# Decoder step on one core: operands of the gated feed-forward layers built from half pairs, squares added by VectorE, later norm products, adding transfers in the last head

## The chip, the cores and the metric

The kernel runs on one NeuronCore of a Trainium2 chip. The metric is the device time of one execution in microseconds, the median of three runs. Everything the kernel does happens on that core's engines: TensorE (PE; its weight loads are shown apart as PEld), VectorE (DVE), ScalarE (ACT), GpSimd (POOL), and SyncE (SP), which mostly starts transfers. Each engine works through its own list of instructions in order. A scheduler fixes that order when the kernel is built, and semaphores hold an instruction until what it needs has been written or released.

## The reference, cut to what matters

The model has two layers with d = 1024. It runs over 512 prompt tokens and 8 × 4 sample tokens with the same weights, so 544 token columns in all.

```python
for i in range(2):
    h = rmsnorm(x, norm_mix[i])
    x = x + (short_conv_mixer(h) if i == 0 else retention_mixer(h))   # x: 544 x 1024
    x = x + swiglu(rmsnorm(x, norm_ffn[i]), w_gate, w_up, w_down)      # 1024 -> 2816 -> 1024
y = rmsnorm(x, final_norm)

def rmsnorm(x, g): return x * rsqrt(mean(x * x, -1) + 1e-6) * g
def swiglu(x, wg, wu, wd): return (silu(x @ wg) * (x @ wu)) @ wd
```

`short_conv_mixer` is a projection to 3 × 1024, a gated convolution of width 3, and a projection back with `conv_w_out`. `retention_mixer` has four heads; each ends in a projection with its part of `ret_w_out`, which is added to x. All of it is float32.

## The kernel before, in words

**Layout.** x stands transposed in eight tiles `x[0]` to `x[7]` of 128 features by 544 tokens. A float32 product is made of three faster ones: each operand is split in a high and a low part (`split`: ScalarE copies to the high part, line 186, VectorE subtracts it to get the low part, line 187), and TensorE adds high·high, low·high and high·low.

**Order of a layer.** The mixer ends in a projection whose result is added to x tile by tile (`residual`, line 267). In layer 0 the order of the tiles is `PAIRED` = 0, 4, 1, 5, 2, 6, 3, 7. In layer 1 it comes from the last head's `out_project`, whose weight pieces 0, 2, 1, 3 carry two tiles each, so 0, 1, 4, 5, 2, 3, 6, 7. Then the feed-forward part `ffn` begins. Its norm's factor is not applied to x: the products are made from x times the gain alone, and the factor `R` is multiplied in later (lines 587 and 589).

**Seven products in place of eight.** A gate or up product of a pair of weight columns is a `Job`: one step of Strassen's scheme in Winograd's form. x is cut in features (tile k with tile k + 4) and in tokens (two halves of 272), and `operands` makes seven operands of 272 columns from each pair: four blocks and three sums or differences of blocks. The list `OPERAND` says which of the seven each product takes. There are four pairs, so a product is four times three matrix instructions of 128 × 272 (line 471). The first job is run as product 1 (`begin`), then 5, 6, 2, 7 (`middle`), product 1 of the next job, then 4 and 3 (`end`). Between products of one job ScalarE copies the running sum out of its bank ("u1", "u2", "u3": a snapshot, line 529) before the next product is added on top of it.

**Building the operands.** For each pair, ScalarE writes gain times x for both tiles into a buffer `f` (line 568), VectorE makes two differences in place (lines 404 and 405), a split of five blocks (1360 columns) follows, then two more differences (407 and 408) and a split of two blocks (544). The work on a pair starts when both its tiles are there. Two buffers `f` take turns.

**The norm.** `square_sum` adds up the squares: ScalarE squares a tile into `sqlast`, and GpSimd adds it to `sqacc` (line 216); the last tile's is added by VectorE (line 212). `rms_scale` is a generator: five small products with a column of `mean_w` (line 245), then a power on GpSimd (line 221), four empty steps, then six products that spread the factor over the partitions (line 225), then a copy to `R` (line 257). `Job.product` of the first job takes one step of it after each pair's three instructions.

**Weights of a job.** `weights7` loads two pieces, makes four differences on VectorE (lines 429 to 432), and splits. Half of each loaded piece gets its low part from an adding transfer: ScalarE writes minus the high part (line 416), and GpSimd's queue starts a transfer that adds the weight from memory to it (line 417). `load_piece(..., adding=True)` does the same for a whole piece of 128 × 1024 with `split_adding`, which the code before never asks for in `out_project`.

**Order by hand.** `tc.issue_after(ins)` makes the scheduler put what follows after a given instruction; other than that the order is the scheduler's.

## Time and profile before

| | |
|---|---|
| median of 3 runs | 1477.4 us (1476.63 to 1478.4) |
| profiled execution, own time | 1477.55 us |
| its span, first to last instruction | 1475.8 us |
| TensorE busy | 1453.5 us, 98% |
| VectorE / ScalarE / GpSimd busy | 963.4 / 627.8 / 150.5 us |
| mean granted TensorE clock | 0.992 |
| feed-forward of layer 0 begins (first line-471 instruction) | 201.63 us |
| feed-forward of layer 1 begins | 1084.47 us |

Times on the trace count from the span's start. A row of the timeline gives the start, the duration, the engine, the line, the operation, and output and input with their sizes. A row of the stretches gives the stretch, its length, the busy time of each engine with the number of instructions in parentheses, the granted clock of TensorE (1.00 is full), the share of the transfer engines and GB/s.

### The profile page before, as it was taken

Reading aid. Unit: us, or ns where it says so; the run is one execution under the profiler, and the core shown is the slowest. Engines: PE = TensorE matmul, PEld = TensorE weight load, DVE = VectorE, ACT = ScalarE, POOL = GpSimd, SP = SyncE. Lnnn points to the kernel's source line nnn. Section 1 sums busy time; section 2 is a strip of 40 time slices with the busy share of each in tenths; the row PEclk is TensorE's granted clock in tenths of the full one; section 3 lists DMA queues with packets and bytes.
Section 4 is the critical chain, followed back from the end, with each engine's and each line's share of the span. In section 5 each row is a group of like instructions: output and inputs, shape, how many; then the busy total and the mean of one; then the engine's idle time right before and its main releaser. Section 6 shows DMA issues by size and latency. Waiting matters only on the chain.

```text
span 1475.8 us, 26203 instructions
## 1 busy us (share of the span) xinstructions
PE 1453.5 (98%) x10920; PEld 1381.1 (94%) x10920; DVE 963.4 (65%) x1472; ACT 627.8 (43%) x914; POOL 150.5 (10%) x180
## 2 busy tenths in 40 slices
PE   9999999999999999999999999999989999999997
PEld 9999989999999999888988988987779999999997
DVE  6645678847749656648546835835788857848645
ACT  5222457626526435241141223224366725526434
POOL 0100131101101003000000000000041101101002
PEclk9999999999999999999999999999989999999999
DMA  6222235635536435237234523713426635536432
GB/s 225 82 91 86 89 100 132 147 115 131 143 106 144 119 81 192 100 115 246 84 126 161 201 86 114 250 51 118 170 77 150 144 115 133 145 102 141 125 80 83
DMA packets 80263, 188.05 MB, mean 127 GB/s; under 512 B 7680, under 2 KB 24960, under 8 KB 80144
## 3 DMA queue, kind: packets, MB, share of 16 engines
q1 hardware_dynamic: 66576, 162.01, 33.6%
q0 software_dynamic: 12704, 23.15, 9.5%
q8 instruction: 85, 1.39, 0.4%
q10 hardware_dynamic: 864, 1.22, 0.2%
q14 instruction: 34, 0.28, 0.1%
HBM read 165.18 MB, written 21.18 MB: 126 GB/s over the span
## 4 chain that ended last, share of the span: by engine, by line
PE 88%; DVE 6%; DMA 1%; ACT 1%; POOL 1%; issue 1%; SPq 0%; DVEq 0%; POOLq 0%; ACTq 0%
PE mm L173 35%; PE sm L471 31%; PE sm L173 8%; PE sm L883 2%; PE sm L884 2%; PE sm L885 2%; PE sm L161 1%; PE sm L163 1%; PE sm L162 1%; DVE S L1115 1%; PE sm L1094 1%; DVE wl L187 1%; DMA w<-in_ffgu_dram 1%; DVE ol L187 1%; DMA S<-in_rets_dram 1%
## 5 line engine op out<-in xcount | busy, mean ns | idle before, releaser
L186 ACT ACTIVATE wh<-w 128x1024 fp32r<-128x1024 f32 (+4 forms) x142 | 132.7, 939 | 369.4 <-PE mm L173 222.4
L471 PE MATMUL sm<-oh,wh 128*128 128x272 f32 x704 | 204.6, 291 | 4.1 <-ACT oh L186 2.5
L471 PE MATMUL sm<-ol,wh 128*128 128x272 f32 x704 | 203.7, 290 | 0.9 <-DVE ol L187 0.9
L471 PE MATMUL sm<-oh,wl 128*128 128x272 f32 x704 | 203.6, 289 | 0.0
L173 PE MATMUL mm<-xh,wh 128*128 128x272 f32 x932 | 195.0, 290 | 0.2 <-ACT wh L186 0.2
L173 PE MATMUL mm<-xh,wl 128*128 128x272 f32 x932 | 192.6, 289 | 0.0
L173 PE MATMUL mm<-xl,wh 128*128 128x272 f32 x932 | 192.0, 287 | 0.0
L187 DVE TENSOR_TENSOR wl<-w,wh 128x1024 fp32r<-128x1024 f32 (+4 forms) x142 | 153.9, 1088 | 28.5 <-ACT wh L186 26.3
L267 DVE TENSOR_TENSOR x<-x,mm 128x544 f32<-128x544 f32 x91 | 65.4, 719 | 139.2 <-PE mm L173 139.1
L471 PE MATMUL sm<-oh,h 128*128 128x272 f32 x528 | 152.5, 289 | 1.3 <-ACT h L186 0.9
L471 PE MATMUL sm<-ol,h 128*128 128x272 f32 x528 | 152.3, 289 | 0.0
L471 PE MATMUL sm<-oh,l 128*128 128x272 f32 x528 | 151.9, 288 | 0.0
L173 PEld LDWEIGHTS mm<-xh,wh 128*128 128x128 f32 x932 | 146.4, 189 | 5.4 <-DVE wl L187 3.4
L173 PEld LDWEIGHTS mm<-xl,wh 128*128 128x128 f32 x932 | 146.0, 188 | 0.1
L173 PEld LDWEIGHTS mm<-xh,wl 128*128 128x128 f32 x932 | 145.3, 188 | 0.3
L471 PEld LDWEIGHTS sm<-oh,wh 128*128 128x128 f32 x704 | 133.8, 190 | 5.9 <-ACT oh L186 2.7
L417 POOL DMA_DIRECT2D wl<-in_ffgu_dram x88 | 76.6, 871 | 595.9 <-ACT wl L416 359.4
L471 PEld LDWEIGHTS sm<-ol,wh 128*128 128x128 f32 x704 | 133.1, 189 | 1.1 <-DVE ol L187 1.1
L471 PEld LDWEIGHTS sm<-oh,wl 128*128 128x128 f32 x704 | 133.6, 190 | 0.0
L414 ACT ACTIVATE wh<-w 128x1024 fp32r<-128x1024 f32 x88 | 93.2, 1059 | 70.7 <-PE sm L471 47.0
L471 PEld LDWEIGHTS sm<-oh,h 128*128 128x128 f32 x528 | 100.1, 190 | 1.8 <-ACT h L186 1.7
L187 DVE TENSOR_TENSOR l<-w,h 128x1024 fp32r<-128x1024 f32 x88 | 83.8, 954 | 24.6 <-ACT h L186 24.3
(258 smaller groups left out, 3115.2 us busy)
## 6 DMA issues: line engine op xcount, KB each, us to landing
w<-in_ffgu_dram SPq DMA_DIRECT2D x88, 512.0 KB, 3.9
wl<-in_ffgu_dram POOLq DMA_DIRECT2D x88, 256.0 KB, 4.6
w<-in_ffdn_dram SPq DMA_DIRECT2D x96, 192.0 KB, 2.5
S<-in_rets_dram SPq DMA_DIRECT2D x16, 1024.0 KB, 7.5
out_rets_dram<-S SPq DMA_DIRECT2D x16, 1024.0 KB, 5.4
w<-in_cvin_dram SPq DMA_DIRECT2D x21, 512.0 KB, 3.3
w<-in_rtqk_dram SPq DMA_DIRECT2D x16, 512.0 KB, 3.6
w<-in_rtv_dram SPq DMA_DIRECT2D x16, 512.0 KB, 3.6
```

Source lines behind the costliest of these rows:

```text
L161: nc.tensor.matmul(out, lh, rh, start=start, stop=False, skip_group_check=True)
L162: nc.tensor.matmul(out, lh, rl, start=False, stop=False, skip_group_check=True)
L173: last_product[0] = nc.tensor.matmul(half(pt, hf)[:, :HT], w[:, c], act[k][:, hf * HT : (hf + 1) * HT], start=(first and k == ks[0] and i ...
L186: h = nc.scalar.activation(dh, src, AF.Copy)
L187: nc.vector.tensor_sub(dl, src, dh.bitcast(F32))
L267: last_residual[0] = nc.vector.tensor_add(xk, xk, p)
L414: nc.scalar.activation(wh, w, AF.Copy)
L417: nc.gpsimd.dma_start(wl[:, n:], src[:, n:], accum_op=ALU.add)
L471: nc.tensor.matmul(out, w[:, c], b[k][:, at, :], start=(first and k == 0 and i == 0), stop=(k == n - 1 and i == 2), skip_group_check=True,)
L883: nc.tensor.matmul(out, xh[kt][:, ts_], wh[:, cw], start=(kt == 0), stop=False)
L884: nc.tensor.matmul(out, xh[kt][:, ts_], wl[:, cw], start=False, stop=False)
L885: nc.tensor.matmul(out, xl[kt][:, ts_], wh[:, cw], start=False, stop=(kt == KT - 1))
```

## The change

Six edits belong together.

1. `operands` is cut in two. `operands_left` works on the first tile of a pair alone: one difference, and a split of operands 0 and 1, which products 1 and 5 take. `operands_rest` works when the second tile is there: two differences and a split of three operands, then one difference and a split of two. `OPERAND` is renumbered to suit. A pair has the same number of columns to split, in three pieces (544, 816, 544) instead of two (1360, 544).
2. The order of tiles in layer 0 becomes 0, 4, 1, 5, 2, 3, 6, 7, so tile 3, the first of the last pair, comes before tiles 6 and 7.
3. All squares are added by VectorE, and the last tile's square is put after the last pair's operands.
4. The norm's small products are taken during products 7, 4 and 3 of the first job and product 1 of the second (not during 5, 6 and 2), each put by hand after its matrix instruction, and nine empty steps instead of four stand ahead of the spreading products.
5. The second job also takes steps of the norm.
6. In the last head's `out_project`, the second to fourth weight piece get their low part by an adding transfer.

```diff
-PAIRED = [0, 4, 1, 5, 2, 6, 3, 7]
+PAIRED = [[0, 4, 1, 5, 2, 3, 6, 7], [0, 1, 4, 5, 2, 3, 6, 7]]
...
+    last_low = [None]
     def split(dh, dl, src):
         h = nc.scalar.activation(dh, src, AF.Copy)
-        nc.vector.tensor_sub(dl, src, dh.bitcast(F32))
+        last_low[0] = nc.vector.tensor_sub(dl, src, dh.bitcast(F32))
         return h
...
-    def rms_scale(sample=False, pt=None):
+    def rms_scale(sample=False, pt=None, rest=4):
...
-        for _ in range(4):
+        for _ in range(rest):
             yield
...
-    def operands(f, oh, ol):
-        nc.vector.tensor_sub(f[:, 4, :], f[:, 1, :], f[:, 0, :])
-        nc.vector.tensor_sub(f[:, 1, :], f[:, 3, :], f[:, 1, :])
-        split(oh[:, 0:5, :], ol[:, 0:5, :], f)
-        nc.vector.tensor_sub(f[:, 0, :], f[:, 3, :], f[:, 4, :])
+    def operands_left(f, oh, ol):
+        nc.vector.tensor_sub(f[:, 1, :], f[:, 4, :], f[:, 0, :])
+        split(oh[:, 0:2, :], ol[:, 0:2, :], f[:, 0:2, :])
+    def operands_rest(f, oh, ol):
+        nc.vector.tensor_sub(f[:, 4, :], f[:, 3, :], f[:, 4, :])
+        nc.vector.tensor_sub(f[:, 0, :], f[:, 3, :], f[:, 1, :])
+        split(oh[:, 2:5, :], ol[:, 2:5, :], f[:, 2:5, :])
         nc.vector.tensor_sub(f[:, 1, :], f[:, 2, :], f[:, 0, :])
-        split(oh[:, 5:7, :], ol[:, 5:7, :], f[:, 0:2, :])
+        return split(oh[:, 5:7, :], ol[:, 5:7, :], f[:, 0:2, :])
...
-    OPERAND = {1: 0, 2: 2, 3: 3, 4: 6, 5: 4, 6: 5, 7: 1}
+    OPERAND = {1: 0, 5: 1, 2: 2, 3: 3, 7: 4, 6: 5, 4: 6}
...
-                    nc.tensor.matmul(
+                    last = nc.tensor.matmul(
...
-                next(self.weave, None)
+                if which not in (5, 6, 2):
+                    with tc.issue_after(last.ins):
+                        next(self.weave, None)
...
-        jobs[0].weave = steps
+        jobs[0].weave = jobs[1].weave = steps
...
-            def operand(k):
-                f = fp.tile([P, 5, HT], F32, tag="f", name=nm("f"))
-                for i in range(2):
-                    nc.scalar.activation(
-                        f[:, 2 * i : 2 * i + 2, :], halves(x[k + i * KP]), AF.Copy, scale=g_ffn(layer, k + i * KP)
-                    )
-                operands(f, oh[k], ol[k])
+            blocks = {}
+            def operand(kt):
+                k = kt % KP
+                if kt < KP:
+                    blocks[k] = fp.tile([P, 5, HT], F32, tag="f", name=nm("f"))
+                f = blocks[k]
+                where = f[:, 0:5:4, :] if kt < KP else f[:, 2:4, :]
+                nc.scalar.activation(where, halves(x[kt]), AF.Copy, scale=g_ffn(layer, kt))
+                return (operands_left if kt < KP else operands_rest)(f, oh[k], ol[k])
...
-            for i, kt in enumerate(PAIRED):
-                if i % 2 == 0:
-                    operand(kt)
-                square_sum(kt, None, last=PAIRED[-1])
+            made = None
+            for kt in PAIRED[layer]:
+                made = operand(kt)
+                with ExitStack() as held:
+                    if kt == KT - 1:
+                        held.enter_context(tc.issue_after(made.ins))
+                        held.enter_context(tc.issue_after(last_low[0].ins))
+                    square_sum(kt, None, add=nc.vector)
...
-            steps = rms_scale()
+            steps = rms_scale(rest=9)
...
-                wh, wl = load_piece(a["rtout"][h, n2], 2 * 4 * P)
+                wh, wl = load_piece(a["rtout"][h, n2], 2 * 4 * P, adding=rest is not None and n2 > 0)
```

More of the change, by code (lines that the diff above doesn't have):

```diff
@@ L393, in hybrid_decode_kernel @@
         wide("m")
-        for n in PAIRED:
+        for n in PAIRED[0]:
             wh, wl = load_piece(a["cvout"][n], KT * P)
```

## The prediction

> **What bounds the kernel now.** I read the page's chain first, then TensorE's waits, then the two stretches in which those waits lie.
>
> ```profile
> PE 88%; DVE 6%; DMA 1%; ACT 1%; POOL 1%; issue 1%; SPq 0%; DVEq 0%; POOLq 0%; ACTq 0%
> PE sm L471 <- ACT oh L186: 2.5, 1, 2.5
> PE mm L225 <- POOL rN L221: 1.7, 1, 1.7
> PE sm L471 <- ACT wh L414: 1.2, 1, 1.2
> ...
> PE sm L471 <- DVE ol L187: 0.9, 1, 0.9
> PE mm L245 <- DVE sqacc L212: 0.8, 1, 0.8
> PE mm L173 <- DVE x L267: 0.7, 1, 0.7
> ```
>
> TensorE is the bound. The instructions that it waits for in this list all stand at the two entries to the feed-forward part. So the change, which alters little else, is worth what these entries lose. How much is that? The stretches, first with all instructions, then with line 471 alone, and the price of a line-471 matmul in a run without waits:
>
> ```profile
> 201.63:218.24 16.61, 13.20 (x84) 12.34 (x82) 8.11 (x14) 8.43 (x12) 6.45 (x4) 0.79 0.36 101
> 1084.47:1105.35 20.88, 15.48 (x86) 14.31 (x85) 16.03 (x26) 12.86 (x19) 7.41 (x5) 0.75 0.32 76
> ...
> 201.63:218.24 16.61, 9.51 (x60) 8.71 (x60) 0.79 0.36 101
> 1084.47:1105.35 20.88, 12.79 (x62) 10.73 (x63) 0.75 0.32 76
> ...
> 230.79 66.28 PE sm L471 x528
> ...
> 30.10 1.02 PE mm L245 x10
> ...
> 32.62 1.52 PE mm L225 x12
> ```
>
> 66.28 / 528 = 0.1255 us. Layer 0's stretch holds 60 matmuls, 7.53 us, and a norm, which in the first layer's unhindered case takes 1.02 + 1.52 = 2.54. Together 10.07 of 16.61 us: **6.54 are lost**. Layer 1's holds 62, 7.78 us, and 2.54: **10.56 are lost**, and the wait of 0.7 for a residual ahead of it makes 11.25. So at most 17.8 us can be won. Part of the loss is the clock, the seventh figure of a row (after the five busy times):
>
> ```profile
> 203.59:207.00 3.41, 2.63 (x22) 2.45 (x21) 1.98 (x5) 2.90 (x4) 0.30 (x1) 1.00 0.43 153
> 207.00:210.42 3.42, 1.68 (x9) 1.36 (x7) 2.38 (x4) 0.00 (x0) 3.32 (x2) 0.50 0.00 1
> 1084.07:1087.48 3.41, 2.19 (x18) 1.97 (x16) 3.41 (x8) 2.67 (x6) 1.39 (x2) 1.00 0.42 68
> 1087.48:1090.90 3.42, 1.29 (x9) 1.08 (x9) 3.42 (x5) 3.15 (x4) 2.65 (x2) 1.00 0.47 162
> 1090.90:1094.31 3.41, 2.17 (x8) 1.85 (x9) 3.41 (x6) 2.26 (x4) 1.12 (x1) 0.53 0.00 0
> 1097.72:1101.14 3.42, 3.42 (x17) 3.42 (x16) 1.06 (x3) 0.94 (x2) 1.16 (x1) 0.50 0.85 177
> ```
>
> After a stretch of 3.41 us in which TensorE was busy for 1.29, the clock is half; after one with 2.19 it was not. It came back at the end of a stretch that was full. In layer 0 the stretch before the drop has 2.63 busy, of which the ten one-column products of the norm make 1.25 and seem not to count.
>
> **The change part by part: VectorE and ScalarE.** In layer 1 VectorE is busy for the whole of 1084.07 to 1094.31 in the rows above (3.41 or 3.42 of each stretch). What one of its steps costs, what GpSimd's adds cost it, and ScalarE's prices:
>
> ```profile
> 1084.84 0.71 DVE L267 TENSOR_TENSOR x<-x,mm 128x544 f32<-128x544 f32 x1
> 1085.47 0.43 DVE L407 TENSOR_TENSOR f<-f 128x272 f32<-128x272 f32 x1
> 1085.82 0.43 DVE L404 TENSOR_TENSOR f<-f 128x272 f32<-128x272 f32 x1
> 1086.88 0.68 DVE L415 TENSOR_TENSOR wl<-w,wh 128x512 fp32r<-128x512 f32 x1
> 1087.48 0.71 DVE L267 TENSOR_TENSOR x<-x,mm 128x544 f32<-128x544 f32 x1
> 1090.75 1.57 DVE L404 TENSOR_TENSOR f<-f 128x272 f32<-128x272 f32 x1
> ...
> 1089.53 2.49 POOL L216 TENSOR_TENSOR sqacc<-sqacc,sqlast 128x544 f32<-128x544 f32 x1 [0.77 <-ACT sqlast L215]
> ...
> L187 DVE TENSOR_TENSOR wl<-w,wh 128x1024 fp32r<-128x1024 f32 x5 | 6.1, 1222 | 0.3 <-ACT wh L186 0.3
> ...
> L568 ACT ACTIVATE f<-x,vec 128x544 f32<-128x544 f32 x8 | 5.8, 744 | 3.4 <-DVE x L267 2.6 <-DVE ol L187 0.7
> L186 ACT ACTIVATE oh<-f 128x1360 fp32r<-128x1360 f32 x4 | 5.3, 1328 | 0.3 <-DVE f L405 0.3
> L215 ACT ACTIVATE sqlast<-x 128x544 f32<-128x544 f32 x6 | 3.9, 650 | 3.8 <-POOL sqacc L216 3.7
> L186 ACT ACTIVATE oh<-f 128x544 fp32r<-128x544 f32 x4 | 2.6, 643 | 0.0
> ```
>
> Start to start, 544 columns take 0.63, 512 take 0.60, 272 take 0.35. An operation that falls beside a GpSimd add is stretched: 1.57 for 0.43. GpSimd's add therefore costs VectorE about 1.14, and costs ScalarE 3.7 us of waiting for the buffer `sqlast`. Six adds by VectorE cost 6 × 0.63 = 3.8 per layer and take away up to 6 × 1.14 = 6.8. A third split per pair adds no columns; I put it at 0.1 per split. So edit 3 helps VectorE as well as ScalarE.
>
> The adding transfers take three splits of 128 × 1024 from VectorE, 3 × 1.13 = 3.4 us, and give ScalarE three copies of about 1.04. Two of these copies fall where ScalarE waits for VectorE's gate products; the third stands behind the last piece's high part at 1066.8, and ends by 1068.3. Then its transfer is due:
>
> ```profile
> wl<-in_ffgu_dram POOLq DMA_DIRECT2D x88, 256.0 KB, 4.6
> ...
> 1065.72 1.04 ACT L186 ACTIVATE wh<-w 128x1024 fp32r<-128x1024 f32 x1
> ```
>
> 256 KB land after 4.6 us; for 512 KB I bound it by 4.6 and 9.2 and take 6. Issued at 1068.4 it lands at 1074.4. TensorE first wants it when the last piece starts, 1084.47, less its 48 matmuls (6.0) and the wait of 0.7: 1077.7; at 9.2 it would be 1077.6, still in time. The first two have over 10 us. On GpSimd's queue these transfers stand ahead of the powers of the last head's norms, but each is issued before its power is wanted. I cost all three at nothing.
>
> **Layer 0, walked through.** The changed kernel's instruction order gives TensorE 96 line-471 matmuls and the five small products ahead of the spreading ones. VectorE's last wait for weights sets its end: it must take a difference of weights that arrive 4.68 us after a buffer is freed, and has tiles 6 and 7 behind it.
>
> ```profile
> 193.15 4.68 DMA w<-in_ffgu_dram
> ...
> 202.59 0.71 DVE L267 TENSOR_TENSOR x<-x,mm 128x544 f32<-128x544 f32 x1
> ...
> 207.10 2.46 POOL L221 TENSOR_TENSOR rN<-rN,expo 128x5 f32<-128x5 f32 x1 [3.21 <-DVE rN L220]
> ```
>
> The buffer was freed at 193.15; with the new order and the prices above I come to 192.2, so the weights are there at 196.9, two differences (1.2) later tile 6 is added at 198.1 to 198.8, then eight steps (0.60, 0.60, 0.35, 0.35, 0.63, 0.35, 0.92, 0.63), and tile 7 at 203.3 (202.59 before). TensorE starts at 201.63 and meets four waits: operand 0 of the last pair, whose high part ScalarE writes late, 0.25; its low part 1.15 (VectorE's step after tile 7, done at 204.6); operand 5 of that pair, after copy 0.74, difference, split 0.64, 0.35; the second snapshot, which stands behind two weight copies of 1.04 on ScalarE, 0.45. The power on GpSimd (2.46 in this layer) starts 0.3 after the small products and runs beside 22 matmuls, 2.76, so about 0.1 is left. Loss: 2.3 in place of 6.54, **4.24 won**. No stretch of 3.41 us lacks more than 1.5 us of work, so the clock should stay.
>
> **Layer 1, walked through.** Here the power was shorter, and the steps behind `R` cost this:
>
> ```profile
> 1097.51 1.37 POOL L221 TENSOR_TENSOR rN<-rN,expo 128x5 f32<-128x5 f32 x1 [0.38 <-DVE rN L220]
> ...
> 1111.52 1.29 DVE L587 TENSOR_TENSOR g<-g,R 128x1088 f32<-128x1088 f32 x1
> ...
> 1112.84 1.12 ACT L588 ACTIVATE g<-g 128x1088 f32<-128x1088 f32 x1 [0.56 <-DVE g L587]
> ```
>
> TensorE starts at 1084.47 - 0.7 = 1083.78: the wait for a residual goes, since VectorE reaches each of the eight residuals at most 0.8 after its product. Tile 7's is added at 1084.05 to 1084.7. Behind it VectorE has, in its order, low parts of 544 and 816 columns, a difference, a square, a difference, 544, a difference, 512 weights, 816, a difference, 1024 weights: with 0.92 for 816 (by columns, from the steps of 272 and 544) and 1.13 for 1024, 6.9 us, and 0.7 of waiting for ScalarE's copies: to 1092.3. TensorE's order then waits four times for this list: 1.9 (low part of pair 2), 2.05 (high part of the last pair's three operands, at 1089.1), 0.6 (weights' low part), 1.25 (low part of the sums of weights). A snapshot costs 0.3. The norm's first step on VectorE (line 222) stands behind ten weight differences until 1100.6; the power (1.37) ends at 1102.1, when TensorE has run out 0.65 earlier. Sum 6.75. The first two waits leave a stretch of 3.41 us with less than 1.5 busy, so by the rows above the clock halves once more, somewhere between 1086.4 and 1089.4, and comes back about 6.8 us later. From 1089.9 on TensorE loses 0.1 per matmul, some 1.2 us, of which over half only fills the later waits: 0.5. Loss 7.25 in place of 11.25, **4.0 won**.
>
> The Trainium skill ("TensorE: Matmul & The Clock Gate", HAM oscillation) says that idle gaps must exceed about 3.4 us before the clock is throttled. By that rule there would be no drop here either, and the time would be 0.5 us lower, 1468.7, inside the forecast's own range; I leave it no more than a quarter of the forecast's chance. The rows speak against it: the clock fell in both layers, and the longest wait of all is 2.5 us.
>
> **Sum.** 4.24 + 4.0 = 8.2 us, off the profiled execution's 1477.55: 1469.35. That execution lies 0.15 above the median of the runs, so 1469.2. The rest is costed at nothing: between the entries the orders agree but for a pair of transposes, and matmuls fill TensorE after them. `R` comes later in matmuls but not in time: the factor is there at 1104.8, and gate times R, silu and times R again need 1.29 + 1.12 + 1.29, until TensorE is at its 125th matmul; the bank that hangs on it is wanted at the 180th.
>
> **The rivals.** *Nearly all of it goes.* If VectorE's list is 2 us shorter than I walked it and the clock stays, layer 1 loses little more than the norm; the bound is 1477.4 - 17.8 = 1459.6, and half the remaining loss gone gives 1464.4. For it: no step of the list need be stretched. Against: the eleven steps listed behind tile 7, which no edit shortens.
>
> *Layer 1 gives nothing.* TensorE's order makes it wait where before it had other products, and the clock is halved for three stretches as before, so the entry only changes its waits. Then layer 0 alone counts: 1477.4 - 4.2 = 1473.2. For it: VectorE is full there before and after.
>
> *It comes back later.* The entry ends earlier, but the next jobs' weights, on a VectorE that is behind, do not, and TensorE waits for them: no change, 1477.4. Against it: in the walk the third job's weights are ready 4 us ahead.
>
> *Slower.* The stretch is not GpSimd's doing but ScalarE's or the transfers', and stays. Then the new adds come on top, in the place that counts: the 14 steps from tile 7 to the last square in layer 1, each 1.14 longer, 16.0 us behind which everything waits: 1477.4 - 8.2 + 16.0 = 1485.2. It decides from 8.2 / 1.14, so 8 stretched steps, on. Against it: the steps from 1084.84 to 1085.82, with ScalarE and transfers busy, have their plain length.
>
> **How the numbers follow.** Chances: the forecast 0.57 (own range 1466.5 to 1471.5), nearly all 0.14, nothing in layer 1 0.18, back later 0.05, slower 0.06. Faster by over 0.2% (3 us, about what a measurement of this kernel can tell) has 0.57 + 0.14 + 0.18 = 0.89; within 0.2% 0.05; slower 0.06. The range leaves out the two last and part of the second: 1463.5 to 1474.
>
> **What would show it.** Right: after the mixer in layer 0, some 35 matmuls of line 476 without a wait over 1.2 us, clock 1.00; GpSimd without line 216 or 218 at the entries; no VectorE step of 272 columns over 0.5; in layer 1, waits of 1 to 2 us for the operands' splits of the last pairs, and a half clock for two stretches; the spreading products' wait under 1 us. Wrong: a wait for the last piece's low part at 1077; a wait at a later job; stretched steps without an add on GpSimd; or a layer 1 as long as before.

## The result, and the profile after

| | before | after |
|---|---|---|
| median, runs of one comparison | 1476.83 us (1476.57 to 1478.4, 6 runs) | 1468.7 us (1467.48 to 1469.63, 6 runs) |
| profiled execution, span | 1475.8 us | 1466.4 us (own time 1468.62) |
| TensorE busy | 1453.5 us | 1449.5 us |
| mean granted clock | 0.992 | 0.996 |

The changed kernel takes 0.9943 of the time before, 95% interval 0.993 to 0.9955: faster by 8.1 us. The profiled spans lie 9.4 apart: the profiled execution before was 0.7 above the median of its six, and an execution's own time exceeds its span by 1.75 before and by 2.22 after. The page of the changed kernel, its line of the chain by engine, and TensorE's waits (us in total, times, longest):

```profile
PE 1449.5 (99%) x10920; PEld 1378.7 (94%) x10920; DVE 959.4 (65%) x1489; ACT 632.1 (43%) x925; POOL 130.5 (9%) x171
PE 90%; DVE 6%; DMA 1%; ACT 1%; POOL 1%; issue 1%; DVEq 0%; POOLq 0%; ACTq 0%
PE sm L476 <- ACT oh L188: 1.7, 1, 1.7
...
PE sm L476 <- DVE ol L189: 1.1, 2, 0.8
...
PE sm L476 <- ACT u L536: 0.8, 1, 0.8
...
PE sm L476 <- ACT g L536: 0.2, 1, 0.2
PE sm L476 <- DVE wl L420: 0.2, 1, 0.2
```

Line 476 is the feed-forward product that was line 471. The waits for the norm (lines 245 and 225 before) and for the last residual are gone; the longest of those for operands fell from 2.5 to 1.7; a wait of 0.8 for a snapshot (`u`) is new. The two stretches that answer to those of before, with all instructions and then line 476 alone:

```profile
201.51:217.35 15.84, 15.44 (x122) 14.82 (x121) 11.53 (x20) 10.40 (x18) 3.28 (x3) 1.00 0.49 128
1080.09:1099.70 19.61, 16.47 (x115) 15.34 (x114) 18.14 (x32) 13.12 (x21) 3.78 (x4) 0.91 0.56 143
...
201.51:217.35 15.84, 14.01 (x97) 12.62 (x98) 1.00 0.49 128
1080.09:1099.70 19.61, 15.38 (x91) 13.22 (x92) 0.91 0.56 143
```

The first row starts 0.14 us ahead of layer 0's first product (201.65). Layer 0's entry does 97 products and the norm, 97 × 0.1255 + 2.54 = 14.71, in 15.70 us: **1.0 us is lost, 6.5 before**. Layer 1's does 91, 11.42 + 2.54 = 13.96, in 19.61: **5.6 are lost, 10.6 before**. A few products are missing from the trace, so these losses are good to some tenths. Where the time was won along the program is seen from three instructions that every kernel here has: the first product of layer 0's first down projection, the first of the last head's projection, and the first of layer 1's first down projection. In the timelines, first before and then of the changed kernel:

```profile
296.91 0.42 PE L173 MATMUL mm<-xh,wh 128*128 128x272 f32 x2
...
1057.44 0.52 PE L173 MATMUL mm<-yh,wh 128*128 128x272 f32 x2 [1.16 <-ACT yh L186]
...
1183.46 0.42 PE L173 MATMUL mm<-xh,wh 128*128 128x272 f32 x2
```

```profile
292.05 0.42 PE L173 MATMUL mm<-xh,wh 128*128 128x272 f32 x2
...
1052.83 0.39 PE L173 MATMUL mm<-yh,wh 128*128 128x272 f32 x1 [1.22 <-ACT yh L188]
...
1174.05 0.42 PE L173 MATMUL mm<-xh,wh 128*128 128x272 f32 x2
```

So layer 0 won 4.86, the heads gave back 0.25, and from the last head's projection into layer 1 it was 126.02 before and 121.22 after, 4.80 won. Behind the third nothing changed: 292.34 and 292.35 to the end of the span.

In layer 0 the clock stayed at 1.00. In layer 1 it fell once, as it did in the last head, where it had not fallen before (PE busy first of the five engines; the seventh figure is the clock):

```profile
1051.00:1054.40 3.40, 2.11 (x14) 1.47 (x12) 2.89 (x8) 1.39 (x4) 0.73 (x1) 1.00 0.80 155
1054.40:1057.80 3.40, 3.22 (x15) 3.22 (x16) 1.43 (x5) 0.00 (x0) 0.00 (x0) 0.52 0.20 39
...
1081.80:1085.20 3.40, 0.84 (x4) 0.41 (x4) 3.40 (x8) 2.11 (x4) 0.00 (x0) 1.00 0.00 0
1085.20:1088.70 3.50, 3.28 (x14) 3.01 (x15) 3.50 (x6) 1.82 (x4) 0.85 (x1) 0.51 0.48 129
```

### The profile page after: what moved, and what is told of

Read it like the earlier page. It is cut to its first block, busy times and chain, and to the rows that moved or that the text cites. A ratio compares the mean times of both kernels' runs of the same rounds, so it can differ in the third digit from the quotient of the medians.

```text
span 1466.4 us, 26224 instructions
## 1 busy us (share of the span) xinstructions
PE 1449.5 (99%) x10920; PEld 1378.7 (94%) x10920; DVE 959.4 (65%) x1489; ACT 632.1 (43%) x925; POOL 130.5 (9%) x171
## 4 chain that ended last, share of the span: by engine, by line
PE 90%; DVE 6%; DMA 1%; ACT 1%; POOL 1%; issue 1%; DVEq 0%; POOLq 0%; ACTq 0%
PE mm L173 37%; PE sm L476 31%; PE sm L173 8%; PE sm L897 2%; PE sm L898 2%; PE sm L899 2%; PE sm L161 1%; PE sm L163 1%; PE sm L162 1%; PE sm L1108 1%; DVE S L1129 1%; DMA w<-in_ffgu_dram 1%; DVE ol L189 1%; DVE wl L189 1%; DMA S<-in_rets_dram 1%
## 5 line engine op out<-in xcount | busy, mean ns | idle before, releaser
L188 ACT ACTIVATE wh<-w 128x1024 fp32r<-128x1024 f32 (+4 forms) x139 | 129.6, 936 | 346.6 <-PE mm L173 223.3
L476 PE MATMUL sm<-oh,wl 128*128 128x272 f32 x704 | 203.3, 289 | 0.2 <-DVE wl L420 0.2
L189 DVE TENSOR_TENSOR wl<-w,wh 128x1024 fp32r<-128x1024 f32 (+4 forms) x139 | 150.2, 1085 | 27.7 <-ACT wh L188 25.4
L476 PEld LDWEIGHTS sm<-oh,l 128*128 128x128 f32 x528 | 99.6, 189 | 0.0
```

What stands on the lines that cost most here:

```text
L188: h = nc.scalar.activation(dh, src, AF.Copy)
L189: last_low[0] = nc.vector.tensor_sub(dl, src, dh.bitcast(F32))
L476: last = nc.tensor.matmul(out, w[:, c], b[k][:, at, :], start=(first and k == 0 and i == 0), stop=(k == n - 1 and i == 2), skip_group_chec ...
```

## The experiments

The table has the three instructions for every kernel, read from its timeline, and the times. "Projection to layer 1" is the third less the second. "Layer 1 alone" is the part of it from layer 1's first feed-forward product on. "Half clock" is the time that TensorE ran at half clock in layer 0's entry, in the last head and in layer 1's entry, added up from the granted clock of stretches of 1.7 us.

| kernel | layer 0's down | projection to layer 1 | layer 1 alone | half clock | span | median of runs | ratio to before (95%) |
|---|---|---|---|---|---|---|---|
| before | 296.91 | 126.02 | 98.99 | 6.8, 0, 10.2 | 1475.8 | 1476.83 | |
| after | 292.05 | 121.22 | 93.96 | 0, 3.4, 3.4 | 1466.4 | 1468.7 | 0.9943 (0.993 to 0.9955) |
| no_adding | 291.94 | 121.13 | 95.10 | 0, 0, 6.8 | 1466.3 | 1468.25 | 0.9936 (0.9923 to 0.9948) |
| no_squares | 295.83 | 121.70 | 93.18 | 3.4, 0, 0 | 1471.0 | 1472.76 | 0.9963 (0.995 to 0.9975) |
| no_norm | 292.67 | 120.97 | 94.90 | 0, 0, 3.4 | 1467.2 | 1471.26 | 0.9962 (0.9948 to 0.9975) |
| no_operands | 294.37 | 121.58 | 95.52 | 0, 0, 3.4 | 1468.9 | 1472.54 | 0.9964 (0.9952 to 0.9977) |
| only_squares | 296.02 | 122.91 | 96.87 | 3.4, 0, 10.2 | 1472.9 | 1475.2 | 0.9988 (0.998 to 0.9997) |
| only_norm | 298.67 | 127.08 | 99.65 | 10.2, 3.4, 10.2 | 1480.1 | 1478.17 | 1.001 (1.0 to 1.0019) |
| only_operands | 297.41 | 123.22 | 95.31 | 6.8, 0, 3.4 | 1474.4 | 1475.96 | 0.9992 (0.9984 to 1.0001) |
| high_first | 291.58 | 120.57 | 94.51 | 0, 0, 3.4 | 1465.6 | 1468.61 | 0.9944 (0.9931 to 0.9957) |
| warm | 291.93 | 119.74 | 94.01 | 0, 0, 0 | 1465.7 | 1467.46 | 0.9934 (0.9922 to 0.9946) |
| tail_first | 291.89 | 120.70 | 94.65 | 0, 0, 6.8 | 1466.2 | 1467.69 | 0.9934 (0.9921 to 0.9948) |
| tail_adding | 291.78 | 117.61 | 91.54 | 0, 0, 0 | 1463.2 | 1465.04 | 0.9918 (0.9905 to 0.9932) |
| piece_adding | 291.66 | 123.59 | 97.53 | 0, 0, 10.2 | 1468.5 | 1471.8 | 0.9961 (0.9947 to 0.9974) |

Ratios are against runs of the kernel before on the same chip. The columns of one execution and the median can part: the profiled executions of no_norm (1469.37) and no_operands (1471.17) were the fastest of five, that of tail_first (1468.43) the slowest of five, that of only_norm (1481.83) the slowest of twelve. One thing in the changed kernel's own profile matters for every comparison with it: its last head lost 1.2 us to half clock (27.26 from the projection to layer 1's first product, 26.03 to 26.07 in the eight kernels without a late residual there, warm apart). Without that its 121.22 would be 120.0. Only_norm's last head lost time to the clock too, the others' did not.

### One edit undone in the changed kernel

**Adding transfers (no_adding).**

```diff
-                wh, wl = load_piece(..., adding=rest is not None and n2 > 0)
+                wh, wl = load_piece(a["rtout"][h, n2], 2 * 4 * P)
```

> The changed kernel with edit 6 alone undone: the last head's weight pieces get their low parts from VectorE again. Theory (four parts that add up): VectorE has three low parts of about 1.2 us more in the last head, 3.4 us in all, and reaches the operands of layer 1 later; the 0.7 us wait at the last piece's residual comes back and the first half of layer 1's operands is late too. Expected 1470.2 us, 1.5 above the changed kernel, all of it between 1040 and 1100 us, layer 0 as in the changed kernel (group-0 down at about 292.2). Rival (VectorE has slack enough there): 1468.7, no difference.

1468.25 us, no difference: the rival. The trace shows why it is even. Layer 1 begins at 1079.13, 26.03 after the projection's first product (27.26 in the changed kernel, whose last head ran one stretch at half clock), and then waits longer, 1.1, 0.9 and 0.9 in place of 0.8, 1.7 and 0.2, and runs 6.8 us at half clock in place of 3.4. Layer 1 alone takes 95.10, 1.1 more than with the transfers (93.96), and the changed kernel's profile lost as much to the clock in its last head. The wait of 0.7 for a residual does not come back, though the theory had it; with the squares alone it is gone too, so it was not the transfers that took it away.

**Squares (no_squares).**

```diff
-                    square_sum(kt, None, add=nc.vector)
+                    square_sum(kt, None)
```

> The changed kernel with edit 3 alone undone: GpSimd adds the squares at both feed-forward entries again. Theory: VectorE's steps beside an add on GpSimd are stretched again from 0.43 to about 1.6 us, and ScalarE waits up to 3.7 us for the buffer of the squares, which stands ahead of the next tile's operands; each entry loses 1.5 to 2.5 us, so 1472.5 us, 3.8 above the changed kernel, half of it by group-0 down of layer 0. Rival (with the operands built early and the last square put behind them, the squares are off the path): 1468.7, the stretched steps are there and nothing waits for them.

1472.76 us, 4.1 above the changed kernel: the size is that of the theory. Layer 0 loses 3.8 of it, more than the half expected; the part from the projection into layer 1 loses 0.5, or 1.7 without the 1.2 that the changed kernel's last head lost to the clock. That part is lost ahead of layer 1, in waits of 1.24 and 0.72 for residuals. TensorE's waits in layer 0, two of VectorE's steps, the group of ScalarE's squares, and the clock:

```profile
204.72 0.39 PE L476 MATMUL sm<-oh,wh 128*128 128x272 f32 x1 [1.63 <-ACT oh L188]
206.30 0.60 PE L476 MATMUL sm<-ol,wh 128*128 128x272 f32 x1 [0.82 <-DVE ol L189]
...
197.95 0.69 DVE L435 TENSOR_TENSOR w<-w,w 128x512 f32<-128x512 f32 x1 [4.01 <-DMA w<-in_ffgu_dram]
...
201.35 1.60 DVE L411 TENSOR_TENSOR f<-f 128x272 f32<-128x272 f32 x1
...
L217 ACT ACTIVATE sqlast<-x 128x544 f32<-128x544 f32 x18 | 11.7, 647 | 3.1 <-DVE sqacc L218 2.4 <-POOL sqacc L218 0.7
...
202.80:206.20 3.40, 1.05 (x7) 0.61 (x5) 3.37 (x7) 2.71 (x4) 0.00 (x0) 1.00 0.10 41
206.20:209.60 3.40, 3.30 (x14) 3.30 (x15) 2.51 (x6) 2.63 (x6) 0.88 (x1) 0.50 0.47 153
```

The stretched step is back (1.60 in place of 0.43, beside a GpSimd add that runs from 201.30). ScalarE's wait for GpSimd is 0.7, not 3.7: that part of the reason did not hold. Another way was not in the theory. VectorE was 1.6 later with the weights' low part after which their buffer is filled anew (line 420, 192.60 for 191.03): ahead of it stood a step that took 1.30 beside an earlier add, in place of 0.68 (line 434). So the transfer of the next weights was issued at 193.31 (191.74 in the changed kernel), and VectorE waited for them until 197.95 (196.02). Of the 2.6 us by which tile 7 is added later (204.90, 202.31), 1.9 come by the weights. What costs is two waits of 2.4 us close together, then half clock for 3.4 us: 14 products where 27 fit.

**Norm (no_norm).**

```diff
-        jobs[0].weave = jobs[1].weave = steps
+        jobs[0].weave = steps
...
-                if which not in (5, 6, 2):
-                    with tc.issue_after(last.ins):
-                        next(self.weave, None)
+                next(self.weave, None)
...
-            steps = rms_scale(rest=9)
+            steps = rms_scale()
```

> The changed kernel with edits 4 and 5 alone undone: the norm's five one-column products follow the first products of the first job, with four empty steps ahead of the spread. Theory: TensorE reaches the first one-column product before the last square is added and waits there 1 to 2 us in each layer, since the last square stands behind the last operands; then the spread waits for GpSimd's power. Expected 1471.5 us, 2.8 above the changed kernel, with a wait at line 242 or 224 of over 1 us in each layer. Rival (TensorE waits for operands anyway, and the norm's products fall into those waits): 1468.7 to 1469.2.

1471.26 us, 2.6 above by the medians. The profiled execution shows 0.7 of it, as two waits for the power, one in each layer, while the wait for a snapshot in layer 0's second job is gone:

```profile
212.23 1.52 PE L227 MATMUL mm<-cb,rN 128*128 128x128 f32 x12 [1.46 <-POOL rN L223]
...
1098.15 1.52 PE L227 MATMUL mm<-cb,rN 128*128 128x128 f32 x12 [0.74 <-POOL rN L223]
```

There is no wait for the last square, which the theory had. The other four runs took 1470.52 to 1473.91 with a mean clock of 0.995 or 0.996 where this one has 0.998; so in them more is lost, with the clock low, at a place that no profile here shows. A mean clock lower by 0.002 to 0.003 over 1470 us is, by estimate, 6 to 9 us more at half clock.

**Operands (no_operands).** The diff takes back edits 1 and 2: `operands` for a whole pair, one `PAIRED` for both layers, the old `OPERAND`. With them goes the second half of edit 3, that the last square is put behind the last operands.

```diff
-            for kt in PAIRED[layer]:
-                made = operand(kt)
...
+            for i, kt in enumerate(PAIRED):
+                if i % 2 == 0:
+                    operand(kt)
+                square_sum(kt, None, last=PAIRED[-1], add=nc.vector)
```

> The changed kernel with edits 1 and 2 alone undone: a pair's operands are built in one go when both tiles are there, in the order of the kernel before; squares on VectorE, late norm and adding transfers stay. Theory (the parts add up, and this one has what is left): 1471.5 us, 2.8 above the changed kernel, split over both entries. Rival 1 (early operands are the gain, the rest only clears the way): 1475 or more, 6 above. Rival 2 (VectorE's load is the bound, not the order): 1469.0.

1472.54 us, 3.8 above: near the theory (2.8), below rival 1. In the profile 2.3 of it lie in layer 0 and 0.4 from the projection into layer 1, 1.6 in layer 1 alone. Layer 1's three longest waits:

```profile
1087.96 0.39 PE L473 MATMUL sm<-oh,wh 128*128 128x272 f32 x1 [2.12 <-ACT oh L188]
1089.76 0.56 PE L473 MATMUL sm<-ol,wh 128*128 128x272 f32 x1 [1.16 <-DVE ol L189]
1094.75 0.40 PE L473 MATMUL sm<-oh,wl 128*128 128x272 f32 x1 [0.69 <-DVE wl L417]
```

Their sum is 4.0; the changed kernel's three longest there make 2.8 (1.73, 0.82, 0.24). Undone one by one the edits cost 0 + 4.1 + 2.6 + 3.8 = 10.5 us by the medians, where they bring 8.1 together. By the ratios to before, which take out the chips' differences, the last three cost 3.0, 2.8 and 3.1, and without the transfers it is 1.0 faster; each ratio's interval is some 3.7 us wide. So it is not shown that the sum is more than the whole.

### One edit alone on the kernel before

> The kernel before with edit 3 alone: VectorE adds all the squares at both feed-forward entries. Undone one at a time in the changed kernel, the squares cost 3.8 us in layer 0 and under 1 us in layer 1, the operands 2.3 and under 1, the norm 0.6 and 0.8. Theory 1 (in layer 0 the parts need each other, in layer 1 they can stand in for each other): alone the squares bring 1.5 to 2.5 us in layer 0 and 3 to 4 in layer 1, 1472 us. Theory 2 (each part brings what its removal cost): 3.8 and 0.7, so 1473 us with layer 0's group-0 down 3.8 earlier than before. Rival (alone it brings nothing, since VectorE pays for the adds): 1477 or later.

> The kernel before with edits 4 and 5 alone: the norm's one-column products and the spread come later. Theory 1: in layer 1 it takes away the 0.8 us wait for the last square and the 1.7 us wait for the power, so 2.5 us there and nothing in layer 0, 1475.0 us. Theory 2 (the waits for operands behind them grow by as much): 1477.5, no difference.

> The kernel before with edits 1 and 2 alone: operands in two parts, the new order in layer 0, the last square behind the last operands; squares on GpSimd, norm products early, no adding transfers in the last head. Theory 1 (parts need each other in layer 0): the stretched steps of VectorE and ScalarE's wait for the buffer of the squares stay, and the late last square now holds the early norm products; 0.5 us won in layer 0, 1 in layer 1, 1476 us. Rival (the split into two parts is the main gain): 1472. Other side: the late last square makes the early norm products wait longer than before, 1479.

The diffs are those above the other way round: `add=nc.vector` at the entries; late weaving with nine empty steps; the two-part operands with the last square held behind them.

Alone they bring 1.7 us (ratio 0.9988, 0.998 to 0.9997), nothing or less (1.001, 1.0 to 1.0019) and 1.0 (0.9992, 0.9984 to 1.0001, which holds no difference): 1.5 in all, where the three together, which is no_adding, bring 9.8 (0.9936). The times expected for the squares (1472) and the norm (1475.0) were missed, the operands' (1476) was met, though not in its places; theory 1 of the squares holds for layer 0 in kind and goes further than I put it: squares 0.9 won, operands 0.5 lost, norm 1.8 lost; squares with operands (no_norm) 4.2 won, squares with norm (no_operands) 2.5, operands with norm (no_squares) 1.1; all three 4.9. In layer 1 squares alone win 3.1 and operands alone 2.8, any two 4.3 to 5.1, all three 4.8. So there they can in part stand in for each other, but for the norm, which alone loses 1.1 (2.5 was expected to be won). These places are those of one execution each: only_norm's was 3.7 above its median, the pairs have the adding transfers too, and all three would make 6.0 without the half clock in the changed kernel's last head.

What goes with the loss in layer 0 is the clock: the entry ran 6.8 us at half clock before, 3.4, 10.2 and 6.8 with squares, norm or operands alone, 0, 0 and 3.4 with two of them, and not at all with the three. The twelve executions of only_norm say the same: the four with a mean clock of 0.99 or 0.991 took 1480.19 to 1481.83, the others, with 0.993 to 0.996, 1475.14 to 1479.55. The kernel with the norm alone, in layer 0:

```profile
209.60:213.00 3.40, 1.96 (x10) 1.37 (x10) 1.83 (x3) 2.39 (x5) 0.86 (x1) 0.95 0.68 186
213.00:216.40 3.40, 3.40 (x18) 3.40 (x17) 1.84 (x3) 0.00 (x0) 0.00 (x0) 0.50 0.41 70
216.40:219.80 3.40, 3.40 (x17) 3.40 (x17) 1.11 (x3) 0.40 (x1) 1.57 (x1) 0.50 0.00 0
```

Its late norm took away layer 0's waits of 0.78 and 1.74 for the square and the power, and left TensorE with waits of 0.76, 0.42 and 1.02 for operands and weights; then it ran full, at half clock, for some 10 us (to 223). The kernel no_operands has the last two of these waits at the same products, as much work in that stretch (1.96 of 3.40), and kept its clock:

```profile
211.10 0.39 PE L473 MATMUL sm<-ol,h 128*128 128x272 f32 x1 [0.42 <-DVE ol L189]
...
212.64 0.40 PE L473 MATMUL sm<-oh,h 128*128 128x272 f32 x1 [1.02 <-ACT h L188]
```

So these two waits alone do not decide it. Whether the wait of 0.76 ahead of them does, or chance from execution to execution, is not shown. An edit that removes one wait of several is worth little as long as the others still bring the clock down.

### What still holds layer 1 up

**Other products first (high_first).** In layer 1 the first job's products 1 and 5 take the weights' high part with all pairs first.

```diff
+            if self.high and which in (1, 5):
+                order.sort(key=lambda ki: ki[1] == 2)
```

> The changed kernel, and in layer 1 the first job's products 1 and 5 take the weights' high part with all four pairs first, the low part last. TensorE then has 25 matrix instructions in place of 13 that need nothing of the last tile ahead of the first one that does. Theory: the two waits there (0.8 and 1.7 us) are what layer 1 still loses, and the half clock that follows them is made by them: some 1.5 us of the waits are filled and the clock stays whole, so 1.5 to 2.5 us are won: 1466.7 us. Rival (VectorE's list is the bound: the low parts come when they come, and TensorE waits for them later instead): within 0.5 us of the changed kernel, 1468.5, with the waits at other instructions. Rival 2 (clock alone): waits stay, 0.7 us won.

1468.61 us: the rival. From tile 7's residual on VectorE to the product that wants the high part of its operands:

```profile
1079.16 0.71 DVE L269 TENSOR_TENSOR x<-x,mm 128x544 f32<-128x544 f32 x1
...
1083.74 0.39 PE L480 MATMUL sm<-oh,wh 128*128 128x272 f32 x1 [1.66 <-ACT oh L188]
```

4.58 us, and the same in the changed kernel (1080.52 to 1085.10). TensorE did more work ahead of it and waited for the same step; layer 1 alone takes 94.51, not less than the 93.96 of the changed kernel.

**The clock alone (warm).** Matrix instructions of no use where TensorE waits.

```diff
+                    if self.high and which == 2 and (k, i) in ((2, 1), (3, 0)):
+                        idle_at(self.spare, 5 if k == 2 else 8, last.ins)
...
+                            idle_at(pts[0][:, 0, :], 8, last_product[0].ins)
```

> The changed kernel with matrix instructions of no use (128 x 128, a constant times itself, into a spare corner of a bank) where TensorE waits: 8 ahead of the last head's first projection (its wait is 1.2 us), and in layer 1 5 and 8 ahead of the two instructions that wait 0.8 and 1.7 us. The order of all the others is the same. Theory (the clock halves after a stretch of 3.4 us with little work in it, 0.84 us in layer 1 and 2.1, part of it transposes, in the last head): both stretches now hold over 2 us of work, the granted clock stays at 1.00 in both places, the layer's next 14 products take 0.125 us in place of 0.2275, 1.4 us in all; of that the low part of the sums of weights, which VectorE finishes at 1088.0, takes back up to 1.2; so 0.2 to 1.4 us in layer 1, and 1.2 in the last head in the executions where the clock falls there: 1467.5 us. Rival 1 (the clock has another cause): half clock at the same places, 1468.7. Rival 2 (the added instructions delay the waiting ones): 1469.5.

In layer 1 these instructions start a new sum in the bank in which product 2 is being summed, so part of that sum is lost; only the time is read. (The Trainium skill says of such a start, in "PSUM — Partial Sum Buffer", "The four PSUM rules", that it makes the open sum's next step overwrite; the runs don't show the mechanism.) The stretches of layer 1:

```profile
1080.71:1084.11 3.40, 3.28 (x29) 3.27 (x29) 3.40 (x7) 2.10 (x4) 0.00 (x0) 1.00 0.02 5
1084.11:1087.51 3.40, 2.48 (x17) 1.93 (x16) 3.40 (x6) 1.95 (x5) 0.86 (x1) 1.00 0.43 82
1087.51:1090.91 3.40, 3.30 (x24) 2.96 (x24) 3.40 (x6) 1.92 (x4) 0.00 (x0) 1.00 0.71 182
...
1087.40 0.39 PE L485 MATMUL sm<-oh,l 128*128 128x272 f32 x1 [0.64 <-DVE l L189]
```

The clock stays at 1.00, here and in the last head: with work in the stretch it did not fall. The time is 1467.46, 1.2 below the changed kernel, which the intervals of the two ratios don't hold apart, and not from layer 1: from its first product to layer 1's down projection it is 94.01 (changed kernel 93.96), since TensorE now waits 0.64 for the low part of the sums of weights. What the profile has won lies in the last head: layer 1 begins 787.38 after layer 0's down projection, where the changed kernel takes 788.04. (From the projection's own first product it is 25.73 in place of 27.26, but that product starts 0.9 later, part of it behind the eight added ones.) VectorE is full (3.40 of 3.40) through all of it, and from tile 7's residual to the product that wants the high part it is 4.59, as before: in layer 1 VectorE's list is the bound, and half a clock is hidden behind it.

**VectorE's list in another order, and shorter.** Tile 7's differences ahead of tile 6's second low part, squares of both behind the low part of the sums (tail_first, on top of high_first); the same and the whole low part of the first weight piece by an adding transfer (tail_adding); that transfer alone on the changed kernel (piece_adding).

```diff
+                    made, last = made
+                    with tc.issue_after(last.ins):
+                        low(blocks[2], oh[2], ol[2], slice(5, 7), slice(0, 2))
+                        low(blocks[3], oh[3], ol[3], slice(2, 5), slice(2, 5))
+                        low(blocks[3], oh[3], ol[3], slice(5, 7), slice(0, 2))
...
+                    with tc.issue_after(made.ins), tc.issue_after(last_l2[0].ins):
+                        square_sum(KT - 2, None, add=nc.vector)
+                        square_sum(KT - 1, None, add=nc.vector)
...
+        if whole:
+            return split_adding(wh, wl, w, src)
```

> The kernel with the high parts first in layer 1's first job, and VectorE's and ScalarE's lists in layer 1 put in the order in which TensorE needs them: tile 7's differences ahead of tile 6's second low part, the squares of tiles 6 and 7 behind the low part of the sums of weights. From the residual of tile 7 to the high part that TensorE waits for, VectorE has 2.55 us of steps in place of 3.2, and up to the low part of the sums 0.64 us less. Theory (VectorE's list sets the end of layer 1's entry): the 1.7 us wait becomes 1.0, the 0.5 us wait goes, 0.8 to 1.3 us are won: 1467.5 us. Rival (its total work is the bound, and the order only moves the wait to another instruction): 1468.6. Other side (the squares now come too late for the norm's products): 1469.5 with a wait at line 247's kind of product.

> The kernel of the reordered lists, and layer 1's first job gets the whole low part of its first weight piece from an adding transfer, which takes 0.6 us from VectorE ahead of the last operands. Theory (VectorE's list sets the end): another 0.6 us, 1467.0 us, with the wait at the weights' low part gone. Rival (ScalarE, which has 0.5 us more to do there and no idle time from 1069 to 1082, is now late with the operands): no gain, 1467.5 to 1468.6.

> The changed kernel, and layer 1's first job gets the whole low part of its first weight piece from an adding transfer; nothing else is edited, VectorE's and TensorE's orders are the scheduler's. In the built program this moves more than the 0.6 us step: the low part of the sums of weights now stands ahead of the residual of tile 6 in VectorE's list, and TensorE has 21 matrix instructions ahead of the first that needs the last pair's operands, where the changed kernel has 13. Theory 1 (that order and the clock that stays whole are what the reordered kernel with the adding transfer won; the hand-made order is not needed): 1465.5 us, at least 2.5 below the changed kernel, with the clock at 1.00 through layer 1's entry. Theory 2 (the hand-made order is needed, the transfer brings its 0.6 us): 1468.0 us, with the clock at half for a stretch. Rival (ScalarE's half microsecond more delays the operands): 1468.7 or later.

The order alone: 1467.69, 1.0 below the changed kernel by the medians, which the intervals don't hold apart. In its profile layer 1 alone is not shorter (94.65, changed kernel 93.96): its wait for the high part fell to 0.75, where 1.0 was expected, but a snapshot (1.02) and the low part of the sums (0.56) were late in turn, and the clock fell. With the transfer: **1465.04 us, 0.9918 of before (0.9905 to 0.9932), the fastest of all**, 2.7 below the order alone, where I had expected 0.6, and 3.7 below the changed kernel. The transfer alone: 1471.8, 3.1 slower than the changed kernel by the medians, 2.7 by the ratios; layer 1 alone takes 97.53, 3.6 more. The rival had allowed for later, but not for this reason: only 0.7 of the waits are for ScalarE's high parts. Stretches from about the entry on, first of the kernel with both, then with the transfer alone:

```profile
1080.78:1084.18 3.40, 3.04 (x22) 2.60 (x21) 3.40 (x8) 3.40 (x7) 0.00 (x0) 1.00 0.31 55
1084.18:1087.58 3.40, 2.99 (x20) 2.31 (x18) 3.40 (x7) 2.04 (x5) 0.85 (x1) 1.00 0.42 136
1087.58:1090.98 3.40, 2.91 (x23) 2.70 (x23) 3.40 (x6) 1.46 (x3) 0.00 (x0) 1.00 0.51 100
```

```profile
1081.71:1085.11 3.40, 2.94 (x21) 2.50 (x20) 3.40 (x7) 2.99 (x6) 0.00 (x0) 1.00 0.00 0
1085.11:1088.51 3.40, 1.66 (x6) 0.80 (x6) 3.40 (x7) 1.51 (x3) 0.85 (x1) 1.00 0.72 177
1088.51:1091.91 3.40, 2.89 (x13) 2.68 (x14) 3.40 (x6) 2.40 (x3) 0.00 (x0) 0.64 0.33 60
1091.91:1095.31 3.40, 3.40 (x16) 3.40 (x17) 2.64 (x6) 0.92 (x2) 0.16 (x1) 0.50 0.70 201
1095.31:1098.71 3.40, 3.40 (x17) 3.40 (x17) 1.56 (x3) 0.40 (x1) 2.06 (x2) 0.50 0.79 178
```

With both, no wait of a product in layer 1's entry is over half a microsecond, no stretch has much under 3 us of work, and the clock is whole. With the transfer alone, in the scheduler's order, six waits of 0.2 to 0.8 lie within 6 us, the last four of them in and behind a stretch with 1.66 busy, and some 10 us at half clock follow, by then with VectorE no longer full, so that nothing hides them. The scheduler's order is not the changed kernel's either: TensorE has 21 products ahead of the first that needs the last pair's operands, where that has 13, and the low part of the sums stands earlier in VectorE's list. What the transfer does in an unchanged order was not run.

## Why the prediction was right, and where it was not

**The sum.** 1469.2 was forecast, 1468.7 came, with layer 0 at 4.86 won (4.24 forecast) and layer 1 with the last head at 4.80 (4.0). Its mechanism, waits shortened at both entries, is what the traces show; the errors are of single terms, and partly cancel. That the time came within 0.5 is in part luck. The profiled spans differ by 9.4, not by the 8.2 of the sum; the medians differ by less, for the reasons given with the result, and layer 1's 4.80 would be 6.0 but for half clock in the last head, which was not forecast.

**VectorE and ScalarE.** Right on VectorE: no 272-column step of the changed kernel's entries takes over 0.44, and with the adds on GpSimd again one takes 1.60. Overstated on ScalarE: its wait for GpSimd came back as 0.7, not 3.7, once the operands were in two parts. Left out: a late VectorE also holds up the transfer of the next weights, by which no_squares has them 1.9 later in layer 0.

**Adding transfers.** Costed at nothing, and no wait for the last piece's low part appears. But the walk through layer 1 used the 3.4 us that they free on VectorE, by the wait of 0.7 that goes; undone, the time is no longer (1468.25), and that wait stays away. With the squares alone it is gone as well (26.04 from the projection to layer 1, no wait for a residual), so this term did not need the transfers.

**Layer 0.** 2.3 forecast lost, 1.0 measured. The term that was mis-sized is the low part of the last pair, 1.15 forecast, 0.26 measured: the weights came 0.95 earlier than I walked it and tile 7 was added at 202.31, not 203.3.

```profile
191.74 4.18 DMA w<-in_ffgu_dram
...
203.71 0.40 PE L476 MATMUL sm<-ol,wh 128*128 128x272 f32 x1 [0.26 <-DVE ol L189]
...
202.31 0.71 DVE L269 TENSOR_TENSOR x<-x,mm 128x544 f32<-128x544 f32 x1
```

The power needed no wait, and the clock held, as forecast. Missed: 0.84 is given back in the second job, where ScalarE copies a snapshot only after a table load (1.28), the silu and a weight copy:

```profile
221.41 1.28 ACT L598 ACT_TABLE_LOAD   x1
222.70 1.12 ACT L598 ACTIVATE g<-g 128x1088 f32<-128x1088 f32 x1
...
225.77 0.39 PE L476 MATMUL sm<-oh,wh 128*128 128x272 f32 x1 [0.84 <-ACT u L536]
```

The prediction costed the later `R` at nothing; without edits 4 and 5 (no_norm) this wait is not there. A wait at a later job was named as a sign of failure; it came, at a tenth of the gain.

**Layer 1.** 7.25 forecast lost, 5.6 measured. The waits, forecast and measured: low part of pair 2, 1.9 and 0.82; high part of the last pair, 2.05 and 1.73; weights' low part 0.6 and 0.22; low part of the sums of weights 1.25 and none; spread 0.65 and none. The list itself was walked well: from tile 7's residual to the product that wants the high part it took 4.58 where 5.05 was forecast. The fourth wait is tied to the clock: it fell once, as forecast, for one stretch and not two, and the 14 products that it slowed by 0.10 each, 1.4 in all, stand where that wait would be. The price of the fall was put at 0.5; warm shows that in layer 1 the half clock costs nothing net, because VectorE's list ends last. The drop in the last head was not forecast at all; it costs 1.2, since from the projection to layer 1 it is 27.26 there and 26.03 to 26.07 in no_adding, no_norm, no_operands and high_first. The same wait was there before (1.16) without a drop.

**The clock.** By the rule of the Trainium skill ("TensorE: Matmul & The Clock Gate", "HAM oscillation — how this bites in real kernels") no drop was to come with waits this short. It came in layer 1 with a longest wait of 1.73 us, and went when the waits were filled: the rows decide against it here. The time that this rule gave, 1468.7, is the one that was measured; that is chance, since the clock fell twice.

**The rivals.** That layer 1 gives nothing is excluded by 4.8 won there. That all of it goes failed because VectorE is full; tail_adding shows that it is within reach, 3.7 lower, once VectorE's list is put in order and shortened together. That the stretch is not GpSimd's is excluded by no_squares. What stays open is where the executions of no_norm and no_operands that were not profiled lose another 0.8 to 4.5 us. A candidate, not shown: their layer 0 has a stretch with 1.94 and 1.96 of 3.40 busy, and after such a stretch only_norm ran 10.2 us at half clock. The mean clock of no_operands, 0.998 in the profile and 0.993 or 0.994 in the four others, is of that size: by estimate 12 to 15 us more at half clock.

## What to carry to other kernels

Edits that each remove one of several neighbouring waits are not worth what they remove one by one: alone these brought 1.7, 1.0 and nothing, the three together 9.8. In layer 0 this went with the clock, which stayed low until enough of the waits had gone. So count the work in each stretch of 3.4 us after the edit (the least time that the clock stayed low here), not only the longest wait; the count warns, it does not decide. Where one engine's list is full, try its order and its length together: the same transfer cost about 3 us without the order and brought 2.7 with it.

## What was not expected of the hardware

The same wait in the last head, 1.2 us behind transposes, halved the clock in the profiles of two kernels out of the thirteen that have it, the changed one and only_norm. The work there is alike: in a stretch of 3.40 that ends 0.1 ahead of the product that waits, TensorE is busy for 2.28 in the changed kernel, 2.35 in only_norm and 2.27 to 2.34 in the others (0.8 of it transposes in the changed kernel). So something else than this sum decides, perhaps where the limits of the chip's own stretch fall; that is inferred, since they can't be seen where the clock doesn't fall. The Trainium skill ("TensorE: Matmul & The Clock Gate", "What's actually happening") has the window run free of the program and differ from run to run, with which this agrees; the same page ("Part 4: PE-mode transpose") has transposes not count as work for the clock, which no run here separates. How long the clock stays low is not fixed either, but it comes in steps: wherever it fell in the table's fourteen kernels, the time at half clock is 3.4, 6.8 or 10.2 us, once, twice or three times 3.4. In only_norm and piece_adding it stayed low for 10.2 though TensorE was full; no run shows what decides that. And the useless instructions of 128 x 128 float32 appear as two each in the trace, 0.12 us apart.
